# The head of a decoder-layer kernel rebuilt: more warm-up products, a 128-row broadcast of c, the second square on DVE, one inverse root for both row blocks, the bias product moved

## The chip, the cores and the metric

The kernel runs on one core of a Trainium2 chip. The metric is the device time of one execution in microseconds (us). The kernel before was timed three times: 330.17, 328.08 and 331.65 us, median 330.17 us. Engines are named as the profile names them: PE is TensorE's matmul, PEld its weight load, DVE is VectorE, ACT is ScalarE, POOL is GpSimd, SP is SyncE, which here only issues DMAs.

## The reference, cut to what matters

```python
def hybrid_layer(x, c, norm_g, w_ada, b_ada, w_in, ...):
    mod = jax.nn.silu(c) @ w_ada + b_ada
    shift, scale, gate = jnp.split(mod, 3, axis=-1)
    h = rmsnorm(x, norm_g) * (1 + scale[:, None, :]) + shift[:, None, :]
    proj = h @ w_in
    q, k, v, g_attn, cb, cc, cx, g_conv, m_attn, m_conv = jnp.split(proj, IN_OFFSETS, axis=-1)
    attn = moba_attention(split_heads(q), split_heads(k), split_heads(v), rel_bias)
    y_attn = (attn * jax.nn.silu(g_attn)) @ w_o_attn
    y_conv = (short_conv(cb, cc, cx, conv_w) * jax.nn.silu(g_conv)) @ w_o_conv
    merged = jax.nn.sigmoid(m_attn) * y_attn + jax.nn.sigmoid(m_conv) * y_conv
    return x + gate[:, None, :] * (merged @ w_out)
```

The shapes are 256 rows, 1024 channels, 8 heads of 128; all in fp32. A last RMSNorm closes the layer. The change touches only what comes before `h @ w_in`: silu(c), the two sums of squares of x, and the scale and shift of the first 128 channels.

## The kernel before, in words

Rows of x lie on the 128 partitions in two blocks, `xx[:, 0]` and `xx[:, 1]`. The wide products take x transposed: channels on partitions in eight tiles of 128 (`xnT`), 256 rows in the free dimension.

The head does this. PE multiplies a tile of ones by itself (`warm`, L139: four products first, six later), a result nobody reads. It spreads c over all partitions with a product of one row of ones and the row c (`crow`, L225, two products of 512 columns into the banks `pc`), transposes a small table of vectors (`pv`, L227), and after the later warm-ups transposes the scaled x (`px`, L212, sixteen transposes) and makes the bias product (`pb`, L265, from the one-hot table, needed only much later). ACT makes sigmoid(c) half by half (`silu_part`, L233), squares each row block with its sum (`square`, L237), scales each block by its inverse root (L252, L255, L258), copies `px` out and applies scale and shift to the first tile (`full_h(0)`, L165, the tile `hf0`). DVE multiplies sigmoid by c (L234), makes the mean of squares (`rms_scale`, L143), copies the vectors (L242 to L245) and takes the dot products of silu(c) with the rows of w_ada (`ada_dot`, L155), which for one tile end in the reduction into `scs` (L158). POOL raises the mean to the power -0.5 (L145), once for each block.

Then comes the slab stage (`passes`, L205): eight tiles of 128 channels against 2048 columns of w_in, summed in eight PSUM banks. Tile 0 is done wholly in plain fp32 from `hf0` and its slab (16 products of 256 columns), the others mostly as three products of split values. After it the value projection, 36 units of 256 columns with the attention heads between them, the merge and the output projection.

The order on each engine is that of the code, since the head and the slab stage are pinned with `keep_in_program_order`. Loads are issued by SP in the order of the code. An fp32 product shows in the trace as two matmul records, a transpose as one.

Of the kernel before, what the change touches and what calls it, by code (L numbers as in the profile page):

```python
# [23 lines left out]
EPS = 1e-6
NEG = -1.0e30
BLK = {n: i * D for i, n in enumerate(("q", "k", "v", "ga", "cb", "cc", "cx", "gc", "ma", "mc"))}
WARM = 4
WARM2 = 6
EARLYC = 2
# [4 lines left out]
CUTS0 = (0, 2, 3, 4)  # L34
# [9 lines left out]
def layer_kernel(ctx: ExitStack, tc, x, c, vec, wp_all, slab_all, onehot, final_g, out):  # L44
    nc = tc.nc
    x, out = x[0], out[0]

    const = ctx.enter_context(tc.tile_pool(name="const", bufs=1))
    big = ctx.enter_context(tc.tile_pool(name="big", bufs=1))
    wp = ctx.enter_context(tc.tile_pool(name="wp", bufs=3))  # L50
    tp = ctx.enter_context(tc.tile_pool(name="tp", bufs=2))
# [33 lines left out]
    crow = big.tile([1, D], F32, tag="GB", name="crow")  # L85
# [4 lines left out]
    mhalf = const.tile([P, 1], F32, name="mhalf")  # L90
# [25 lines left out]
    pin(nc.sync.dma_start(crow, c))  # L116
# [8 lines left out]
    nc.vector.memset(ones, 1.0)  # L125
# [5 lines left out]
    nc.gpsimd.memset(rv[:, 0:127], NEG)  # L131
    warmup = const.tile([P, 1], F32, name="warmup")
    pin(nc.scalar.activation(warmup, mhalf, AF.Sigmoid))
# [6 lines left out]

    def rms_scale(ss, name):
        ms = tp.tile([P, 1], F32, tag="ms", name=name + "m")
        pin(nc.vector.tensor_scalar(ms, ss, 1.0 / D, EPS, op0=ALU.mult, op1=ALU.add))  # L143
        r = tp.tile([P, 1], F32, tag="rs", name=name + "r")
        nc.gpsimd.tensor_tensor(r, ms, mhalf, op=ALU.pow)  # L145
        return r
# [77 lines left out]
    for n in range(2):  # L224
        pin(nc.tensor.matmul(pc[n], ones[0:1, :], crow[:, n * 512:(n + 1) * 512], start=True, stop=True))  # L225
# [5 lines left out]
    def silu_part(n):  # L231
        cols = slice(n * 512, (n + 1) * 512)
        pin(nc.scalar.activation(csb[:, cols], pc[n], AF.Sigmoid))  # L233
        pin(nc.vector.tensor_mul(csb[:, cols], csb[:, cols], pc[n]))  # L234

    def square(t):
        pin(nc.scalar.activation(xx[:, 2 + t, :], xx[:, t, :], AF.Square, accum_out=ss[:, t:t + 1]))  # L237

    silu_part(0)
    square(0)  # L240
    r0 = rms_scale(ss[:, 0:1], "r0")
    pin(nc.vector.tensor_copy(vT, pv[:, 0:56]))  # L242
    modb = vT[:, 8:24].rearrange("p (k s) -> p k s", s=2)
    pin(nc.vector.scalar_tensor_tensor(modb[:, :, 1], modb[:, :, 1], 1.0, vT[:, 0:KT], op0=ALU.add, op1=ALU.mult))
    pin(nc.vector.tensor_copy(parts[:, :, :, 4], modb))  # L245
    silu_part(1)
    square(1)
    dot = ada_dot(0, CUTS0, 256)
    run(dot, EARLYC)
    r1 = rms_scale(ss[:, 1:2], "r1")  # L250
    run(dot)
    pin(nc.scalar.activation(xx[:, 2, :], xx[:, 0, :], AF.Copy, scale=r0))  # L252
    for k in range(2):
        xn_trans(0, k)
# [9 lines left out]
    pb = wt[0:NH, P:512]  # L264
    pin(nc.tensor.matmul(pb, oneh[:, 3 * P:], oneh[:, 0:3 * P], start=True, stop=True))  # L265
# [409 lines left out]
```

## Time and profile before

| what | value |
|---|---|
| median of three timed runs | 330.17 us (328.08 to 331.65) |
| profiled execution, first to last instruction | 329.4 us |
| PE busy | 321.4 us, 98% |
| DVE busy | 247.3 us, 75% |
| ACT busy | 189.0 us, 57% |
| POOL busy | 5.6 us, 2% |

The profile is of one execution. It gives the span of 329.4 us and no other time for that execution. A busy PE in it is not a PE at its peak: the ends of pipelined matmuls are modelled, so the distance from one start to the next tells more than a duration.

### The profile page before, as it was taken

The numbers are of one execution on the slowest core, as the hardware profiler recorded it, in microseconds if no ns is written. First come the engines' busy times: TensorE is split into PE (matmuls) and PEld (weight loads), VectorE is DVE, ScalarE is ACT, GpSimd is POOL, SyncE is SP. The second block draws the span as 40 slices with busy tenths as digits, with TensorE's granted clock in tenths as the row PEclk, the third lists the DMA queues.
The fourth block names the chain that finished last, engine by engine and source line by source line (L and its number), as shares of the span: only waits on it lengthen the run. The fifth ranks groups of instructions, "written<-read, shape, count | busy, mean of one in ns | idle before, by whom it ended". The sixth has DMA issues, their size and how long they took to land.

```text
span 329.4 us, 4903 instructions
## 1 busy us (share of the span) xinstructions
PE 321.4 (98%) x1870; PEld 281.9 (86%) x1870; DVE 247.3 (75%) x452; ACT 189.0 (57%) x305; POOL 5.6 (2%) x14
## 2 busy tenths in 40 slices
PE   8999999999999999999999999999999999999992
PEld 5689999988888888988888888888888888888892
DVE  2799993476388779697776998999946466787764
ACT  5654555364578676784768574856465635443430
POOL 3000000000000000000000000000000000000010
PEclk9999999999999999999999999999999999999998
DMA  6999999885645434543454469659875665400003
GB/s 240 406 409 403 410 412 352 309 303 214 247 150 200 171 129 141 211 160 127 137 206 169 142 217 373 225 193 370 346 294 205 228 218 202 182 0 2 0 0 127
DMA packets 14264, 72.75 MB, mean 221 GB/s; under 512 B 1523, under 2 KB 2819, under 8 KB 8098
## 3 DMA queue, kind: packets, MB, share of 16 engines
q1 hardware_dynamic: 12658, 70.40, 57.4%
q10 hardware_dynamic: 1488, 1.97, 1.9%
q8 instruction: 14, 0.23, 0.3%
q0 software_dynamic: 96, 0.09, 0.1%
q14 instruction: 8, 0.07, 0.1%
HBM read 71.39 MB, written 1.06 MB: 220 GB/s over the span
## 4 chain that ended last, share of the span: by engine, by line
PE 93%; DMA 2%; DVE 2%; ACT 1%; POOL 1%; SPq 0%; issue 0%; POOLq 0%; DVEq 0%; ACTq 0%
PE acc L205 15%; PE aoa L340 5%; PE acx L340 5%; PE aoc L340 5%; PE acb L340 5%; PE agc L340 5%; PE aga L340 4%; PE amc L340 4%; PE ama L340 4%; PE acc L340 4%; PE aoc L341 2%; PE aoa L341 2%; PE acx L341 2%; PE acc L341 2%; PE acb L341 2%; PE amc L341 2%
## 5 line engine op out<-in xcount | busy, mean ns | idle before, releaser
L205 PE MATMUL acc<-hf,slab 128*128 128x256 f32 x60 | 16.1, 418 | 0.0
L205 PEld LDWEIGHTS acc<-hf,slab 128*128 128x128 f32 x60 | 12.2, 213 | 3.0 <-ACT H L270 1.3
L155 DVE CUSTOM_DVE_ANT_0 ada<-ada,csb,vT 128x512 f32<-128x512 f32 (+1 forms) x18 | 12.3, 687 | 0.0
L155 DVE CUSTOM_DVE_ANT_0 ada<-ada,csb 128x512 f32<-128x512 f32 (+1 forms) x18 | 11.2, 626 | 0.5 <-DMA ada<-in_wp_dram 0.5
L407 DVE CUSTOM_DVE_ANT_0 L<-pS,BI 128x128 f32<-128x128 f32 x8 | 2.3, 292 | 12.2 <-PE pS L404 12.2
L306 DVE TENSOR_SCALAR QK<-acc 128x512 f32<-128x512 f32 x2 | 1.4, 686 | 9.1 <-PE acc L205 9.1
L572 POOL TENSOR_TENSOR rf<-ms,mhalf 128x1 f32<-128x1 f32 x2 | 1.7, 826 | 306.1 <-DVE ms L597 302.5
L554 ACT ACTIVATE SQ<-TT 128x512 f32<-128x512 f32 x3 | 1.9, 626 | 7.6 <-DVE TT L549 7.6
L304 ACT ACTIVATE QK<-acc 128x512 f32<-128x512 f32 x4 | 2.2, 601 | 7.0 <-PE acc L205 7.0
L377 DVE CUSTOM_DVE_ANT_0 gate<-gate,csb,vT 128x512 f32<-128x512 f32 x8 | 6.0, 744 | 0.3 <-DMA gate<-in_wp_dram 0.3
L139 PE MATMUL wt<-ones 128*128 128x128 f32 x20 | 5.0, 437 | 1.0 <-DVE parts L127 1.0
L340 PE MATMUL aoa<-GA,oa0h 128*128 128x512 f32 x16 | 5.8, 404 | 0.0
L340 PE MATMUL aoa<-GA,oa1h 128*128 128x512 f32 x16 | 5.7, 399 | 0.0
L340 PE MATMUL aoc<-GC,oc2h 128*128 128x512 f32 x16 | 5.7, 399 | 0.0
L340 PE MATMUL aoc<-GC,oc1h 128*128 128x512 f32 x16 | 5.7, 399 | 0.0
L340 PE MATMUL aoa<-GA,oa3h 128*128 128x512 f32 x16 | 5.7, 399 | 0.0
L340 PE MATMUL acx<-H,cx0h 128*128 128x512 f32 x16 | 5.7, 398 | 0.0
L340 PE MATMUL aoc<-GC,oc0h 128*128 128x512 f32 x16 | 5.7, 398 | 0.0
L340 PE MATMUL aoa<-GA,oa2h 128*128 128x512 f32 x16 | 5.7, 398 | 0.0
L340 PE MATMUL aoc<-GC,oc3h 128*128 128x512 f32 x16 | 5.7, 398 | 0.0
L340 PE MATMUL acc<-H,cc0h 128*128 128x512 f32 x16 | 5.7, 398 | 0.0
L340 PE MATMUL acb<-H,cb0h 128*128 128x512 f32 x16 | 5.7, 398 | 0.0
(460 smaller groups left out, 1221.9 us busy)
## 6 DMA issues: line engine op xcount, KB each, us to landing
slab<-in_slab_dram SPq DMA_DIRECT2D x16, 512.0 KB, 10.2
ada<-in_wp_dram SPq DMA_DIRECT2D x15, 512.0 KB, 10.2
wv<-in_wp_dram SPq DMA_DIRECT2D x4, 1024.0 KB, 10.6
wcc<-in_wp_dram SPq DMA_DIRECT2D x4, 1024.0 KB, 4.8
wcx<-in_wp_dram SPq DMA_DIRECT2D x4, 1024.0 KB, 4.8
wcb<-in_wp_dram SPq DMA_DIRECT2D x4, 1024.0 KB, 4.8
wgc<-in_wp_dram SPq DMA_DIRECT2D x4, 1024.0 KB, 4.8
wga<-in_wp_dram SPq DMA_DIRECT2D x4, 1024.0 KB, 4.9
```

The lines of the kernel that those rows point to most:

```text
L139: pin(nc.tensor.matmul(wt[:, 0:P], ones, ones, start=True, stop=True))
L155: pin(nc.vector.tensor_tensor_reduce(src, src, csb[:, k:k + n], vT[:, i:i + 1] if s else 1.0, 0.0, ALU.mult, ALU.add, parts[:, i, s, k // ...
L205: pin(nc.tensor.matmul(acc[j // 2][:, (j % 2) * S:(j % 2 + 1) * S], w[i][:, j * P:(j + 1) * P], x, start=(i == 0 and j // 2 not in opened) ...
L304: pin(nc.scalar.activation(dst, src, AF.Copy, scale=scale))
L306: pin(nc.vector.tensor_scalar_mul(dst, src, scale))
L340: nc.tensor.matmul(a, hi[:, k, cols], rhs[:, k, :], start=(k == 0), stop=False)
L341: nc.tensor.matmul(a[:, S:], lo[:, k, cols], rhs[:, k, 0:S], start=False, stop=(k == KT - 1))
L377: nc.vector.tensor_tensor_reduce(src, src, csb[:, q * 512:(q + 1) * 512], 1.0, 0.0 if q else vT[:, 24 + b:25 + b], ALU.mult, ALU.add, gpar ...
L407: nc.vector.tensor_tensor_reduce(L[:, 0:P], pS[:, 0:P], BI[:, h, 0:P][:, ::-1], 1.0, -3.0e38, ALU.add, ALU.max, mx[:, 0:1])
L554: nc.scalar.activation(SQ[:, t, 0:w], TT[:, t, cols], AF.Square, accum_out=s8[:, slot:slot + 1])
L572: nc.gpsimd.tensor_tensor(r, ms, mhalf, op=ALU.pow)
```

## The change

`WARM` goes from 4 to 8 and `WARM2` from 6 to 12; a constant `WARM3` is added that nothing uses. `crow` becomes a tile of 128 rows, cleared by DVE, and c is loaded into its row 0 by ACT's queue and not by SP's; the broadcast multiplies all 128 rows. The square of block 0 stays on ACT and goes ahead of the first sigmoid; that of block 1 becomes one `tensor_tensor_reduce` on DVE. One mean and one power operation of two columns serve both blocks, ahead of the dot products. The vectors are copied by ACT and finished by three POOL operations. The load of tile 0's modulation weights is cut in two and not three, its dot products are 512 columns wide. The bias product is 258 columns wide and stands after the first two transposes.

```diff
-WARM = 4
-WARM2 = 6
-EARLYC = 2
+WARM = 8
+WARM2 = 12
+WARM3 = 2
-CUTS0 = (0, 2, 3, 4)
+CUTS0 = (0, 2, 4)
...
-    crow = big.tile([1, D], F32, tag="GB", name="crow")
+    crow = big.tile([P, D], F32, tag="GB", name="crow")
-    mhalf = const.tile([P, 1], F32, name="mhalf")
+    mhalf = const.tile([P, 2], F32, name="mhalf")
...
-    pin(nc.sync.dma_start(crow, c))
+    nc.vector.memset(ones, 1.0)
+    pin(nc.vector.memset(crow, 0.0))
...
+    pin(nc.scalar.dma_start(crow[0:1, :], c))
...
-        pin(nc.tensor.matmul(pc[n], ones[0:1, :], crow[:, n * 512:(n + 1) * 512], start=True, stop=True))
+        pin(nc.tensor.matmul(pc[n], ones, crow[:, n * 512:(n + 1) * 512], start=True, stop=True))
...
+    pin(nc.scalar.activation(xx[:, 2, :], xx[:, 0, :], AF.Square, accum_out=ss[:, 0:1]))
     silu_part(0)
-    square(0)
-    r0 = rms_scale(ss[:, 0:1], "r0")
-    pin(nc.vector.tensor_copy(vT, pv[:, 0:56]))
+    pin(nc.vector.tensor_tensor_reduce(xx[:, 3, :], xx[:, 1, :], xx[:, 1, :], 1.0, 0.0, ALU.mult, ALU.add, ss[:, 1:2]))
+    ms2 = tp.tile([P, 2], F32, tag="ms2", name="ms2", bufs=1)
+    pin(nc.vector.tensor_scalar(ms2, ss, 1.0 / D, EPS, op0=ALU.mult, op1=ALU.add))
+    r01 = tp.tile([P, 2], F32, tag="r01", name="r01", bufs=1)
+    pin(nc.gpsimd.tensor_tensor(r01, ms2, mhalf, op=ALU.pow))
+    silu_part(1)
+    pin(nc.scalar.activation(vT, pv[:, 0:56], AF.Copy))
     modb = vT[:, 8:24].rearrange("p (k s) -> p k s", s=2)
-    pin(nc.vector.scalar_tensor_tensor(modb[:, :, 1], modb[:, :, 1], 1.0, vT[:, 0:KT], op0=ALU.add, op1=ALU.mult))
-    pin(nc.vector.tensor_copy(parts[:, :, :, 4], modb))
-    silu_part(1)
-    square(1)
-    dot = ada_dot(0, CUTS0, 256)
-    run(dot, EARLYC)
-    r1 = rms_scale(ss[:, 1:2], "r1")
-    run(dot)
-    pin(nc.scalar.activation(xx[:, 2, :], xx[:, 0, :], AF.Copy, scale=r0))
+    pin(nc.gpsimd.tensor_scalar_add(modb[:, :, 1], modb[:, :, 1], 1.0))
+    pin(nc.gpsimd.tensor_mul(modb[:, :, 1], modb[:, :, 1], vT[:, 0:KT]))
+    pin(nc.gpsimd.tensor_copy(parts[:, :, :, 4], modb))
+    run(ada_dot(0, CUTS0, 512))
+    pin(nc.scalar.activation(xx[:, 2, :], xx[:, 0, :], AF.Copy, scale=r01[:, 0:1]))
     for k in range(2):
         xn_trans(0, k)
-    pin(nc.scalar.activation(xx[:, 3, 0:256], xx[:, 1, 0:256], AF.Copy, scale=r1))
+    pb = wt[0:NH, P:512]
+    pin(nc.tensor.matmul(pb[:, 126:], oneh[:, 3 * P:], oneh[:, 126:3 * P], start=True, stop=True))
+    pin(nc.scalar.activation(xx[:, 3, 0:256], xx[:, 1, 0:256], AF.Copy, scale=r01[:, 1:2]))
...
-    pb = wt[0:NH, P:512]
-    pin(nc.tensor.matmul(pb, oneh[:, 3 * P:], oneh[:, 0:3 * P], start=True, stop=True))
```

How the instructions stand, first on PE from its first product to the first slab product (`wt` is the bank of the warm-ups and of the bias product, `acc` the slab stage's). Before:

```order
L139 MATMUL wt<-ones 128x128 x4
L225 MATMUL pc_131<-crow,ones 128x512
L225 MATMUL pc_132<-crow,ones 128x512
L227 MATMUL pv<-ident,vecs 128x56
L139 MATMUL wt<-ones 128x128 x6
L212 MATMUL px_137<-ident,xx 128x128 x4
...
L212 MATMUL px_140<-ident,xx 128x128 x2
L265 MATMUL wt<-oneh 8x384
L205 MATMUL acc_206<-hf_194,slab_95 128x256 x2
```

PE at the same place now:

```order
L140 MATMUL wt<-ones 128x128 x8
L219 MATMUL pc_135<-crow,ones 128x512
L219 MATMUL pc_136<-crow,ones 128x512
L221 MATMUL pv<-ident,vecs 128x56
L140 MATMUL wt<-ones 128x128 x12
L206 MATMUL px_141<-ident,xx 128x128 x2
L248 MATMUL wt<-oneh 8x258
L206 MATMUL px_141<-ident,xx 128x128 x2
...
L206 MATMUL px_144<-ident,xx 128x128 x2
L199 MATMUL acc_209<-hf_197,slab_95 128x256 x2
```

The warm-ups double on both sides of the broadcast, and the bias product leaves the place right ahead of the first slab product.

DVE from its first wait on ACT to the dot products of tile 0, before (`ISA` is a reducing product, the row after it reads its sum):

```order
L234 TENSOR_TENSOR csb<-csb,pc_131 128x512
L143 TENSOR_SCALAR r0m<-ss 128x1
L242 COPY vT<-pv 128x56
...
L234 TENSOR_TENSOR csb<-csb,pc_132 128x512
L155 ISA ada_91,parts<-ada_91,csb 128x256
...
L143 TENSOR_SCALAR r1m<-ss 128x1
L155 ISA ada_91,parts<-ada_91,csb,vT 128x256
```

DVE at the same place now:

```order
L228 TENSOR_TENSOR csb<-csb,pc_135 128x512
L232 ISA xx,ss<-xx 128x1024
L232 ISA ss 128x1
L234 TENSOR_SCALAR ms_161<-ss 128x2
L228 TENSOR_TENSOR csb<-csb,pc_136 128x512
L149 ISA ada_92,parts<-ada_92,csb 128x512
```

The mean of block 1 no longer stands behind the first dot products, which wait for a load; a square of 1024 columns now stands between the first half of silu(c) and both means. On all engines the instructions after the first slab product stand as before.

## Rows read from the trace of the kernel before

**Rows 1.** The page: its first line, the busy time of each engine, the clock row (40 equal slices, tenths of full speed), and the shares of the engines in the chain that ended last.

```profile
span 329.4 us, 4903 instructions
...
PE 321.4 (98%) x1870; PEld 281.9 (86%) x1870; DVE 247.3 (75%) x452; ACT 189.0 (57%) x305; POOL 5.6 (2%) x14
...
PEclk9999999999999999999999999999999999999998
...
PE 93%; DMA 2%; DVE 2%; ACT 1%; POOL 1%; SPq 0%; issue 0%; POOLq 0%; DVEq 0%; ACTq 0%
```

**Rows 2.** What PE waited for in the whole run (the waits of engine PE: total us, times, longest us).

```profile
PE wt L139 <- DVE parts L127: 1.0, 1, 1.0
PE px L212 <- ACT xx L255: 0.7, 1, 0.7
```

**Rows 3.** The chain of waits that ended last, pieces of the first 20 us (start us, us, what).

```profile
0.73 0.34 SPq L116
...
2.00 6.81 DMA ada<-in_wp_dram
...
9.62 0.08 DVE r1m L143
...
9.77 0.73 POOL r1r L145
...
10.52 0.52 ACT xx L255
...
11.08 3.25 PE px L212 x14
14.33 1.37 PE wt L265 x2
```

**Rows 4.** PE in order of time (start us, us, line, what, count): the head; then the slab stage in a window from 15.6 to 19.5 us, then in one from 19.5 to 24.4 us, whose first record began at 19.21.

```profile
1.04 2.08 PE L139 MATMUL wt<-ones 128*128 128x128 f32 x8 [1.04 <-DVE parts L127]
3.05 3.78 PE L225 MATMUL pc<-crow,ones 1*128 1x512 f32 x4
...
7.04 2.93 PE L139 MATMUL wt<-ones 128*128 128x128 f32 x12
9.76 0.63 PE L212 MATMUL px<-ident,xx 128*128 128x128 f32 x2
...
15.63 4.09 PE L205 MATMUL acc<-hf,slab 128*128 128x256 f32 x9
...
19.21 5.48 PE L205 MATMUL acc<-hf,slab 128*128 128x256 f32 x24
24.34 0.47 PE L205 MATMUL acc<-H,slab1h 128*128 128x256 f32 x1
```

**Rows 5.** ACT in order of time in the head.

```profile
0.72 1.28 ACT L133 ACT_TABLE_LOAD   x1 [0.72 <-PEq L664]
...
5.16 0.60 ACT L233 ACTIVATE csb<-pc 128x512 f32<-128x512 f32 x1 [2.94 <-PE pc L225]
...
8.40 1.14 ACT L252 ACTIVATE xx<-xx,r0r 128x1024 f32<-128x1024 f32 x1
...
10.94 0.92 ACT L258 ACTIVATE xx<-xx,r1r 128x768 f32<-128x768 f32 x1
11.81 0.60 ACT L217 ACTIVATE xnT<-px 128x512 f32<-128x512 f32 x1
12.44 0.60 ACT L165 ACTIVATE hf<-xnT,scs 128x256 f32<-128x256 f32 x1
```

**Rows 6.** DVE in order of time in the head (means, products, and the first and last operation of the dot products of tile 1); then groups of DVE's instructions by form in the first 40 us (count, busy us, mean ns).

```profile
5.79 0.69 DVE L234 TENSOR_TENSOR csb<-csb,pc 128x512 f32<-128x512 f32 x1 [4.75 <-ACT csb L233]
6.82 0.15 DVE L143 TENSOR_SCALAR r0m<-ss 128x1 f32<-128x1 f32 x1 [0.35 <-ACT xx L237]
...
15.31 0.69 DVE L155 CUSTOM_DVE_ANT_0 ada<-ada,csb 128x512 f32<-128x512 f32 x1
...
18.00 0.16 DVE L158 TENSOR_REDUCE scs<-parts 128x2 f32<-128x10 f32 x1
...
L155 DVE CUSTOM_DVE_ANT_0 ada<-ada,csb 128x512 f32<-128x512 f32 x10 | 6.8, 684 | 0.0
...
L155 DVE CUSTOM_DVE_ANT_0 ada<-ada,csb 128x256 f32<-128x256 f32 x4 | 1.6, 422 | 0.5 <-DMA ada<-in_wp_dram 0.5
...
L125 DVE MEMSET ones<- 128x128 f32 x1 | 0.2, 165 | 0.8 <-PEq L664 0.8
...
L126 DVE MEMSET mhalf<- 128x1 f32 x1 | 0.1, 59 | 0.0
```

**Rows 7.** DMA issues of the first 60 us: count, KB each, median us from issue to landing.

```profile
xx<-in_x_dram SPq DMA_DIRECT2D x2, 512.0 KB, 3.3
...
oneh<-in_onehot_dram POOLq DMA_DIRECT2D x1, 49.0 KB, 6.7
vecs<-in_vec_dram POOLq DMA_DIRECT2D x1, 28.0 KB, 4.3
```

**Rows 8.** Later in the slab stage, in order of time: ACT's split tile 1 of h, the last slab's split, and PE at that slab.

```profile
18.19 0.60 ACT L165 ACTIVATE H<-xnT,scs 128x256 fp32r<-128x256 f32 x1 [0.66 <-DVE scs L158]
...
51.02 1.06 ACT L187 ACTIVATE slab7h<-slab 128x1024 fp32r<-128x1024 f32 x1 [0.48 <-ACT hf L165]
...
61.98 3.04 PE L205 MATMUL acc<-H,slab7h 128*128 128x256 f32 x24
```

More of the change, by code (lines that the diff above doesn't have):

```diff
@@ L124, in layer_kernel @@
         load_ktile(i)
-    nc.vector.memset(ones, 1.0)
     nc.vector.memset(mhalf, -0.5)
@@ L131, in layer_kernel @@
     nc.gpsimd.memset(rv[:, 0:127], NEG)
+    pin(nc.scalar.dma_start(crow[0:1, :], c))
     warmup = const.tile([P, 1], F32, name="warmup")
-    pin(nc.scalar.activation(warmup, mhalf, AF.Sigmoid))
+    pin(nc.scalar.activation(warmup, mhalf[:, 0:1], AF.Sigmoid))
     wt = bank("wt")
@@ L139, in warm @@
             pin(nc.tensor.matmul(wt[:, 0:P], ones, ones, start=True, stop=True))
[L141 to L146, printed above, removed]
     def ada_dot(i, cuts, n):
@@ L234, in silu_part @@
         pin(nc.vector.tensor_mul(csb[:, cols], csb[:, cols], pc[n]))
-    def square(t):
-        pin(nc.scalar.activation(xx[:, 2 + t, :], xx[:, t, :], AF.Square, accum_out=ss[:, t:t + 1]))
+    pin(nc.scalar.activation(xx[:, 2, :], xx[:, 0, :], AF.Square, accum_out=ss[:, 0:1]))
     silu_part(0)
-    square(0)
-    r0 = rms_scale(ss[:, 0:1], "r0")
-    pin(nc.vector.tensor_copy(vT, pv[:, 0:56]))
-    modb = vT[:, 8:24].rearrange("p (k s) -> p k s", s=2)
-    pin(nc.vector.scalar_tensor_tensor(modb[:, :, 1], modb[:, :, 1], 1.0, vT[:, 0:KT], op0=ALU.add, op1=ALU.mult))
-    pin(nc.vector.tensor_copy(parts[:, :, :, 4], modb))
-    silu_part(1)
-    square(1)
-    dot = ada_dot(0, CUTS0, 256)
-    run(dot, EARLYC)
-    r1 = rms_scale(ss[:, 1:2], "r1")
-    run(dot)
-    pin(nc.scalar.activation(xx[:, 2, :], xx[:, 0, :], AF.Copy, scale=r0))
+    pin(nc.vector.tensor_tensor_reduce(xx[:, 3, :], xx[:, 1, :], xx[:, 1, :], 1.0, 0.0, ALU.mult, ALU.add, ss[:, 1:2]))
[5 more added lines that the diff above has]
+    pin(nc.scalar.activation(vT, pv[:, 0:56], AF.Copy))
+    modb = vT[:, 8:24].rearrange("p (k s) -> p k s", s=2)
+    pin(nc.gpsimd.tensor_scalar_add(modb[:, :, 1], modb[:, :, 1], 1.0))
[3 more added lines that the diff above has]
+    pin(nc.scalar.activation(xx[:, 2, :], xx[:, 0, :], AF.Copy, scale=r01[:, 0:1]))
     for k in range(2):
         xn_trans(0, k)
-    pin(nc.scalar.activation(xx[:, 3, 0:256], xx[:, 1, 0:256], AF.Copy, scale=r1))
+    pb = wt[0:NH, P:512]
+    pin(nc.tensor.matmul(pb[:, 126:], oneh[:, 3 * P:], oneh[:, 126:3 * P], start=True, stop=True))
+    pin(nc.scalar.activation(xx[:, 3, 0:256], xx[:, 1, 0:256], AF.Copy, scale=r01[:, 1:2]))
     for k in range(2):
         xn_trans(1, k)
-    pin(nc.scalar.activation(xx[:, 3, 256:], xx[:, 1, 256:], AF.Copy, scale=r1))
+    pin(nc.scalar.activation(xx[:, 3, 256:], xx[:, 1, 256:], AF.Copy, scale=r01[:, 1:2]))
     xn_copy(0)
@@ L571, in finish @@
         r = tp.tile([P, 1], F32, tag="rs", name=f"rf{t}")
-        nc.gpsimd.tensor_tensor(r, ms, mhalf, op=ALU.pow)
+        nc.gpsimd.tensor_tensor(r, ms, mhalf[:, 0:1], op=ALU.pow)
         pregain(t, cols, src)
```

## The prediction

> **What bounds the kernel now.** I read the page first: PE is busy for 321.4 of 329.4 us and holds 93% of the chain that ended last [rows 1]. Then the waits of PE: two in the whole run, 1.0 us at the start and 0.7 us before the transposes [rows 2]. So once PE has begun the slab stage at 15.63 it does not stop for anything until the output, and what the head can give is the time at which PE is through with slab 0, which was 24.34 [rows 4]. Whatever that moves, the rest should move with it, as long as the producers keep ahead.
>
> They do. Tile 1 of h stood split at 18.19 + 0.60 = 18.79 against its first use at 24.34, and the last slab's split at 51.02 + 1.06 = 52.08 against a use of that slab from 60 to 65 [rows 4, 8]. The lead is 5.5 us at the start and grows. A PE that comes 4 us earlier still finds its data. The dot products of tile 1 (from 15.31 on DVE) stand behind the same work as before, so tile 1 comes at about the old time; this 18.8 is the floor for the end of slab 0.
>
> Next the chain of the head [rows 3]: the load of the first modulation weights until 8.8, two dot products on DVE, and only behind them the mean of block 1 (9.62), its power on POOL (9.77), the scaling on ACT (10.52), fourteen transposes (11.08 to 14.33), the bias product (1.37 us), and the slab stage. The change attacks all of it but the load.
>
> Last the clock. The clock row says full speed in all but the last slice [rows 1], but the starts do not agree. In slab 0 the first eight records start (19.21 - 15.63) / 8 = 0.447 us apart, the next 24 (24.34 - 19.21) / 24 = 0.214 apart [rows 4]: one instruction at the two levels, 1.2 and 2.4 GHz. The head is all at the lower one: 0.251 us for each of the first eight warm-up records (1.04 to 3.05), 0.227 for each of the twelve later ones (7.04 to 9.76), 0.945 for each of the four of the broadcast. Between those warm-ups stood 3.8 us in which only one row of the array worked, and the clock did not rise. It rose some 3.6 to 4 us into the slab products, which use all rows without a gap.
>
> **The change part by part.**
>
> *Warm-ups and broadcast.* Sixteen records at 0.227 to 0.251 from 1.04 on end at 4.7 to 5.05; I take 4.85. Then the broadcast, if c is there. Now it uses 128 rows, so full-row products run without a gap from 1.04 on, and by the delay at slab 0 the clock rises near 5. Before, the first half of the broadcast reached ACT 5.16 - 3.05 = 2.11 us after its start [rows 4, 5]. At the higher level it is half, about 1.05. I take 1.6, between the two, since one rise in one run does not fix its moment: first half at 6.45, against 5.16 before. This part loses 1.3 us, because the warm-ups ahead of c are longer.
>
> *c by ACT's queue.* The load waits for DVE's clearing of `crow`, and the table load and the first square are queued behind it on ACT. The clearing: 0.165 us for 128 columns and 0.059 for one [rows 6] make (0.165 - 0.059) / 127 a column, 0.9 us for 1024; at worst eight times 0.165, 1.3. So it is issued at 1.9 to 2.3. To landing: no more than 2.3 us for the same row before (0.73 to 3.05), 3.3 for x, 4.3 for the vectors [rows 3, 4, 7]. That is 4.2 to 6.6; it is nearest to the same row, so 4.2 to 4.6, just ahead of PE at 4.85. ACT's table load (1.28 us) then ends near 3.7 and the first square (two of x at 3.3 us, now issued first) near 5.3: hidden behind the broadcast.
>
> *Squares, mean, power.* From 6.45: sigmoid to DVE 0.63 (5.16 to 5.79), product 0.69, square of 1024 columns. The same kind of operation takes 422 ns for 256 and 684 for 512 columns [rows 6], so 1.21 for 1024, 1.25 with its reading; mean 0.15; power 0.73, with gaps 0.8. Both roots stand at 9.9. Then ACT scales block 0, 1.14, the first part of block 1, 0.42 (10.52 to 10.94), the rest 0.87 (10.94 to 11.81), copies the transposed x, 0.63, and makes `hf0`, 0.60 [rows 3, 5]: 11.05, 11.5, 12.35, 13.0, 13.6.
>
> *Dot products.* Beside this DVE does the second half of silu(c), 0.69, and four dot products of 512 columns: tile 1's took 18.00 - 15.31 = 2.69, the reduction 0.16 [rows 6]. From 9.15 that is 12.7, ahead of 13.0: hidden by 0.3 us. If that cover went, each further us of it would show whole. The three POOL operations on the vectors have no row like them; between DVE's 0.15 and POOL's 0.73 each they end at 10.4 to 12.1, behind the power in POOL's queue, before the reduction that waits for them. ACT's copy of the vectors falls in its wait for the roots. Two loads for three change no time that anyone waits for, as the last dot products began after 11 before and do now.
>
> *Transposes and bias product.* Fourteen transposes took 3.25 [rows 3]. From 11.5 they end at 14.75 at the old pace, at 13.1 at half; with the clock up I take the half, hidden behind `hf0`. The bias product (1.37 us on the chain) now falls in PE's wait between the two scalings, and its table, among POOL's first instructions and 6.7 us to landing [rows 7], is there before that.
>
> *Slab 0.* It starts at 13.6, 2.0 us earlier, and takes 32 x 0.214 = 6.85 us, not 8.71: 1.9 us. It ends at 20.45, after the floor of 18.8. The sum is 24.34 - 20.45 = 3.9 us. Bounds: broadcast wholly at the higher level 0.55 more, wholly at the lower 0.5 less; transposes at the old pace 14.75 + 6.85 = 21.6, 2.7 us in all. So 2.7 to 4.45.
>
> One rule speaks against leaning on this. The Trainium skill, "TensorE: Matmul & The Clock Gate", Part 4: PE-mode transpose, says that a transpose does not count as a busy PE for the clock. The trace agrees: PE worked without a gap from 11.08, on transposes and a small product, and slab 0 still began at the lower level. By that rule nothing after the last warm-up holds the clock up until slab 0; it is the second rival.
>
> **The rivals.**
>
> *Slower: the clock does not rise in the head.* c fills one row, the other 127 of the broadcast are zeros, and if such a product, or the switching of weights between the products of ones, does not count, all added PE work is done at 1.2 GHz: 4.85 + 3.78 + 0.3 + 24 x 0.227 + 16 x 0.232 + 0.9 = 19.0 for the start of slab 0, and 8.71 more: 27.7, 3.4 us later than now, 332.8. For it: 2.0 and 2.7 us of the same warm-ups did not raise the clock. Against it: now they are 3.8 and, with the broadcast, over 7 us. It decides at a rise later than 16: slab 0 then starts at (19.0 + 16) / 2 = 17.5 and ends 6.85 later, at the old 24.34.
>
> *The clock rises and falls again before slab 0.* From about 10.4 (6.45, 0.95 for the second half, 0.3, 24 x 0.114) to 13.6 PE has transposes, one small product and waits. If that loses the higher level, transposes end at 14.75 and slab 0 at 23.5: 0.9 us gained, 328.5. For it: in the trace the clock row falls in the last slice, after PE's end, and transposes never raised it. Against it: that fall shows only with PE wholly idle.
>
> *c lands late, or the doubled warm-ups leave a gap after all.* With 6.2 in place of 4.2 PE stands for 1.4 us, the broadcast's first half comes at 8.3, `hf0` at 15.4, and slab 0 at the higher level ends at 22.3: 2.0 gained, 327.4; with the rise late as well, about 1 gained.
>
> *It does less than it says:* if PE had waits after 24.34 that the trace gives as work, the gain would stop there. Nothing speaks for that but the modelled ends; I leave it in the remainder.
>
> **How the numbers follow.** The forecast has 0.60, the fall 0.13, late c 0.12, no rise 0.10, the rest 0.05. Against the profiled 329.4 the forecast is 325.5; the median of the runs shown is 0.8 higher, which gives 326.3. I put 326.0. The range reaches from 329.4 - 4.45, 325, with a little for the spread of the runs, 324.8, to the two middle rivals, 328.5 with the 0.8, rounded to 329.5; that holds the forecast, the fall and the late c, 0.85. One per cent, what a measurement of this kernel can tell from no change, is 3.3 us: 326.9 and 333.5. The forecast's 2.7 to 4.45 lies astride the first, some three quarters of it beyond: 0.45 for faster. A quarter of the forecast, the fall, late c and most of the rest are no change: 0.44. No rise, 332.8 to 333.6, with the remainder: 0.11 slower.
>
> **What would show it.** Warm-up records 0.25 apart that fall to about half near 5 to 8 us, and the later 24 within 3 us; broadcast starting at 4.8 to 5 with no gap; the one power operation at 9.1; slab 0 from 13.6, all 32 records 0.214 apart, done near 20.5; no new wait of PE behind it. Wrong would be: warm-ups at 0.227 to the end and slab 0 at 19, the no-rise rival; slab 0 beginning with records 0.45 apart after fast warm-ups, the fall; a wait of PE for `crow`, the late load; a wait of PE at tile 1 or later, which would say that the lead was not what I read.

## The result, and the profile after

The changed kernel takes 331.51 us (median of 20 runs, 329.79 to 333.39), the kernel before 329.45 us (20 runs, 327.0 to 333.46). The ratio is 1.0078 with a 95% interval of 1.0052 to 1.0104: slower, by 2.1 us between the medians, and within about one per cent, where 326.0 was forecast. The first lines of its page, against [rows 1]:

```profile
span 329.7 us, 4933 instructions
...
PE 319.6 (97%) x1890; PEld 280.9 (85%) x1890; DVE 248.2 (75%) x443; ACT 188.6 (57%) x304; POOL 6.8 (2%) x16
...
PEclk9899999999999999999999999999999999999999
...
PE 94%; DMA 1%; issue 1%; DVE 1%; ACT 0%; POOL 0%; POOLq 0%; ACTq 0%
```

PE is busy 1.8 us less and the span is 0.3 us longer. The clock row has a dent in its second slice that [rows 1] lacks. What PE waited for, against [rows 2]:

```profile
PE pc L219 <- DMA crow<-in_c_dram: 2.6, 1, 2.6
PE wt L140 <- DVE ones L116: 1.0, 1, 1.0
```

The broadcast waits 2.6 us for c. The chain of waits shows what stands ahead of it (start us, us, what):

```profile
1.15 0.91 DVE crow L117
...
2.09 4.90 DMA crow<-in_c_dram
...
7.13 3.48 PE pc L219 x4
```

The clearing takes the 0.91 us that was forecast, but the load of one row lands at 6.99, not at 4.2 to 4.6. PE in order of time (start us, us, line, what, count; the row of the slab stage is from a window of 12 to 21 us, the last from the view of one tile, whose columns are durations min/median/max in ns and first to last start in us):

```profile
1.04 3.45 PE L140 MATMUL wt<-ones 128*128 128x128 f32 x16 [1.04 <-DVE ones L116]
7.13 3.48 PE L219 MATMUL pc<-crow,ones 128*128 128x512 f32 x4 [2.64 <-DMA crow<-in_c_dram]
...
10.82 2.94 PE L140 MATMUL wt<-ones 128*128 128x128 f32 x24
...
14.56 1.75 PE L206 MATMUL px<-ident,xx 128*128 128x128 f32 x14
...
16.32 5.01 PE L199 MATMUL acc<-hf,slab 128*128 128x256 f32 x22
...
L199 PE MATMUL acc<-H,slab1h x24: 278/283/467, 23.1 to 28.8; 128*128 128x256 f32 x24
```

The sixteen early warm-ups end at 4.49, PE stands until 7.13, and the broadcast then takes 3.48 us, little less than the 3.78 of [rows 4]. The trace's clock record says why: the clock rose at 3.99, fell at 7.41 and rose again at 10.82. One stretch of the table by windows (columns: PE, PEld, DVE, ACT, POOL busy and counts, clock, DMA share, GB/s) has it at the lower level, with PE busy throughout:

```profile
7.41:10.82 3.41, 3.41 (x6) 0.85 (x4) 1.25 (x2) 0.77 (x2) 0.00 (x0) 0.50 1.00 379
```

Slab 0 then starts at 16.32, and slab 1 at 23.14, 1.2 us ahead of the 24.34 of [rows 4]. That lead does not reach the end: from there to the end of the span it is 306.5 us, against 305.1 before. PE has no further wait, so only its pace can have eaten it. In the 36 units each pair of products has 512 and 256 columns. Here are the products of 512 columns of two units in the kernel before (gc2 and mc3), then of the same two and of oc3 in the changed one:

```profile
L340 PE MATMUL agc<-H,gc2h x16: 392/394/395, 177.9 to 183.1; 128*128 128x512 f32 x16
L340 PE MATMUL amc<-H,mc3h x16: 392/394/395, 250.0 to 255.2; 128*128 128x512 f32 x16
```

```profile
L332 PE MATMUL agc<-H,gc2h x16: 395/398/403, 176.6 to 181.9; 128*128 128x512 f32 x16
L332 PE MATMUL amc<-H,mc3h x16: 395/398/403, 250.1 to 255.4; 128*128 128x512 f32 x16
...
L332 PE MATMUL aoc<-GC,oc3h x16: 395/398/403, 295.4 to 300.7; 128*128 128x512 f32 x16
```

From gc2 to mc3, thirteen units of the same work, it is 72.1 us before and 73.5 now. The lead of 1.3 us at gc2 is gone at mc3. By the starts in the trace a pair takes 346.5 ns in one kernel and 353.3 in the other, all the way from gc1 to oa0: 83.3 against 84.9 us, 1.6 us. So two things are to be explained: a head that came 2.7 us later than forecast, and a later pace that nobody had touched.

### The profile page after: what moved, and what is told of

It reads as the page before. It is cut to its first block, busy times and chain, and to the rows that moved or that the text cites. A ratio compares the mean times of both kernels' runs of the same rounds, so it can differ in the third digit from the quotient of the medians.

```text
span 329.7 us, 4933 instructions
## 1 busy us (share of the span) xinstructions
PE 319.6 (97%) x1890; PEld 280.9 (85%) x1890; DVE 248.2 (75%) x443; ACT 188.6 (57%) x304; POOL 6.8 (2%) x16
## 3 DMA queue, kind: packets, MB, share of 16 engines
HBM read 71.39 MB, written 1.06 MB: 220 GB/s over the span
## 4 chain that ended last, share of the span: by engine, by line
PE 94%; DMA 1%; issue 1%; DVE 1%; ACT 0%; POOL 0%; POOLq 0%; ACTq 0%
PE acc L199 15%; PE ama L332 5%; PE amc L332 5%; PE aoc L332 5%; PE aoa L332 5%; PE aga L332 5%; PE acx L332 5%; PE agc L332 5%; PE acc L332 5%; PE acb L332 4%; PE acx L333 2%; PE ama L333 2%; PE aoc L333 2%; PE aoa L333 2%; PE aga L333 2%; PE amc L333 2%
## 5 line engine op out<-in xcount | busy, mean ns | idle before, releaser
L149 DVE CUSTOM_DVE_ANT_0 ada<-ada,csb,vT 128x512 f32<-128x512 f32 x16 | 12.0, 749 | 0.0
L149 DVE CUSTOM_DVE_ANT_0 ada<-ada,csb 128x512 f32<-128x512 f32 x16 | 11.0, 688 | 0.0
L159 ACT ACTIVATE H<-xnT,scs 128x256 fp32r<-128x256 f32 x7 | 4.2, 604 | 5.8 <-DVE scs L152 5.8
L140 PEld LDWEIGHTS wt<-ones 128*128 128x128 f32 x40 | 6.0, 240 | 1.1 <-DVE ones L116 1.0
L332 PE MATMUL agc<-H,gc1h 128*128 128x512 f32 x16 | 5.8, 404 | 0.0
L332 PE MATMUL agc<-H,gc2h 128*128 128x512 f32 x16 | 5.7, 399 | 0.0
L332 PE MATMUL aga<-H,ga1h 128*128 128x512 f32 x16 | 5.7, 399 | 0.0
L332 PE MATMUL ama<-H,ma0h 128*128 128x512 f32 x16 | 5.7, 399 | 0.0
L332 PE MATMUL ama<-H,ma3h 128*128 128x512 f32 x16 | 5.7, 399 | 0.0
L332 PE MATMUL amc<-H,mc2h 128*128 128x512 f32 x16 | 5.7, 399 | 0.0
```

What stands on the lines that cost most here:

```text
L140: pin(nc.tensor.matmul(wt[:, 0:P], ones, ones, start=True, stop=True))
L149: pin(nc.vector.tensor_tensor_reduce(src, src, csb[:, k:k + n], vT[:, i:i + 1] if s else 1.0, 0.0, ALU.mult, ALU.add, parts[:, i, s, k // ...
L159: pin(nc.scalar.activation(dst, xnT[:, i, :], AF.Identity, scale=scs[:, i, 1:2], bias=scs[:, i, 0:1]))
L332: nc.tensor.matmul(a, hi[:, k, cols], rhs[:, k, :], start=(k == 0), stop=False)
```

## The experiments

Two theories stood at first: the late c (the head decides) and the pace (the stretch from gc1 on decides). The rival to both was that the two profiles were just unlike executions.

**The two kernels, looked at again** (before_again and after_again are copies, no edit).

> The kernel before, unchanged, for a second trace of it. Theory 'pace' (after the head PE falls into one of two paces, 346.5 or 353.5 ns for a pair of products of 512 and 256 columns, and which stretch runs at which pace differs from one execution to the next): slab 1 begins within 1.5 us of 24.3, yet the stretch from the first gc1 product to the first oa0 product is either 83.3 us, as in the first trace, or 84.9, and the span differs from 329.4 by the sum of such differences. Theory 'late c' (all that matters is when slab 0 is done): the span less the start of slab 1 is again 305.1 within 0.3.

> The changed kernel, unchanged, for a second trace. Both theories: the row c lands near 7.0 again, 4.9 us after its issue, and PE waits about 2.6 us for it. 'Pace': the span less the start of slab 1 (306.6 in the first trace) differs by up to 2 us between the two traces of the same program. 'Late c': it is 306.6 within 0.3, and the time varies with the clock in the head alone.

Medians 331.0 (327.15 to 331.97) and 331.74 (330.45 to 333.81) against 329.52 for the kernel before on the same chip: ratios 1.0028 (0.9983 to 1.0073) and 1.009 (1.0057 to 1.0124). The stretch from gc1 to oa0 was 83.3 and 84.9 us again. The pace belongs to the program, not to the execution. The clock of the head does not: in after_again it did not rise until 12.45, and slab 0 began at 17.08, not at 16.32.

**c first, one row** (c_first_row: the changed kernel with c back at the front of SP's queue and the broadcast of one row).

```diff
-    crow = big.tile([P, D], F32, tag="GB", name="crow")
+    crow = big.tile([1, D], F32, tag="GB", name="crow")
-    pin(nc.vector.memset(crow, 0.0))
+    pin(nc.sync.dma_start(crow, c))
-    pin(nc.scalar.dma_start(crow[0:1, :], c))
-        pin(nc.tensor.matmul(pc[n], ones, crow[:, n * 512:(n + 1) * 512], start=True, stop=True))
+        pin(nc.tensor.matmul(pc[n], ones[0:1, :], crow[:, n * 512:(n + 1) * 512], start=True, stop=True))
```

> The changed kernel with c loaded as one row by SP ahead of all other loads and the broadcast made from that one row, as before the change; warm-ups, square on DVE, one root, bias product as changed. 'Late c': c lands by 3, PE starts the broadcast at 4.5 without a wait, the first half reaches ACT at about 6.6 or, at the higher clock, 5.6, the first slab product starts at 13 to 14 in place of 16.3, slab 1 begins at 20 to 22 in place of 23.1, and the median falls 1.5 to 3 us below the changed kernel's. 'Pace': the head ends as early as that, but the median moves by less than 1 us, as the stretches after it run at the slow pace. A third reading, that one-row products lose the clock: the first slab records are 0.45 apart and slab 1 begins at 22 to 23.

PE in order of time, and a stretch by windows:

```profile
4.48 1.98 PE L218 MATMUL pc<-crow,ones 1*128 1x512 f32 x4
...
6.59 4.57 PE L139 MATMUL wt<-ones 128*128 128x128 f32 x24
...
13.61 0.70 PE L198 MATMUL acc<-hf,slab 128*128 128x256 f32 x2
```

```profile
7.54:10.96 3.42, 3.42 (x18) 3.42 (x18) 2.35 (x7) 1.81 (x3) 1.37 (x4) 0.50 1.00 393
```

The gap is gone and slab 0 starts at 13.61, as forecast for the change itself. Yet the median is 331.18 (328.71 to 331.71), ratio 1.0037 (0.9992 to 1.0083): the spans lie at 326.8 to 327.2 in three executions, the traced one among them, and at 329.3 to 329.8 in seven. The stretch from gc1 to oa0 is again 84.9. The clock fell from 7.54 to 10.96 although PE had no gap.

**c by 128 rows of DMA** (c_wide: each partition loads c, no broadcast on PE, both sigmoids ahead of the first square, 20 and 4 warm-ups).

```diff
-    pin(nc.vector.memset(crow, 0.0))
+    pin(nc.sync.dma_start(crow, bass.AP(tensor=c.tensor, offset=c.offset, ap=[[0, P], [1, D]])))
...
-WARM = 8
-WARM2 = 12
+WARM = 20
+WARM2 = 4
```

> The changed kernel with c loaded on all 128 partitions by SP ahead of all other loads (0.5 MB), no broadcast on PE, warm-ups 20 and 4. 'Late c': sigmoid of c starts near 3.7, the roots stand near 8.5, the first slab product starts near 12 and slab 1 begins at 19 to 20, four us earlier than in the changed kernel; the median is 325.5 to 327.5. 'Pace': slab 1 as early, the median above 328.

332.19 (331.44 to 333.42), ratio 1.0088 (1.0052 to 1.0123). The load puts 512 KB ahead of x; the square of block 1 waited for x until 8.1, and PE stood 2.85 us before the first transposes:

```profile
12.07 0.44 PE L205 MATMUL px<-ident,xx 128*128 128x128 f32 x2 [2.85 <-ACT xx L240]
...
13.39 3.25 PE L205 MATMUL px<-ident,xx 128*128 128x128 f32 x14
```

The clock fell at 12.43, and the fourteen transposes went at the lower level. In this form, with the tiles at their lower place and 20 and 4 warm-ups, a wide load saves nothing against the changed kernel's 331.74.

**What sets the pace: the place of tiles.** Against the kernel before, the changed one has every tile of one pool that is made after the head (hf, low, E, ET, L, cc, cx, y) 64 bytes lower in SBUF, since two small tiles of one buffer each stand in the place of two with two buffers each. Five runs take this apart. b_sbuf is the kernel before with that shift alone, its order of work kept:

```diff
+    ms2 = tp.tile([P, 2], F32, tag="ms2", name="ms2", bufs=1)
+    r01 = tp.tile([P, 2], F32, tag="r01", name="r01", bufs=1)
     def rms_scale(ss, name):
-        ms = tp.tile([P, 1], F32, tag="ms", name=name + "m")
+        t = int(name[1])
+        ms = ms2[:, t:t + 1]
...
-        r = tp.tile([P, 1], F32, tag="rs", name=name + "r")
+        r = r01[:, t:t + 1]
```

> The kernel before with one edit: the two inverse roots write two columns of shared tiles, so that the pool's later tiles (hf, low, E, ET, L, cc, cx, y) lie 64 bytes lower in SBUF, as they do in the changed kernel; the order of the work is that of before. The head should stay as it was: slab 1 from about 24.2. Theory layout (where the tiles lie sets which of two paces PE falls into after the attention's last product): gc1 to oa0 takes 84.9 us instead of 83.3, time about 331 to 332. Theory entry (how long the program before it is, and when the stretch is entered, sets the pace): 83.3, time that of before, 329.5. Theory chance (each execution falls anew into either pace): either, and the spread of the executions is that of before, 326.9 to 331.6.

a_layout is the changed kernel with the shift taken back:

```diff
-    ms2 = tp.tile([P, 2], F32, tag="ms2", name="ms2", bufs=1)
+    ms2 = tp.tile([P, 2], F32, tag="ms2", name="ms2", bufs=2)
...
-    r01 = tp.tile([P, 2], F32, tag="r01", name="r01", bufs=1)
+    r01 = tp.tile([P, 2], F32, tag="r01", name="r01", bufs=2)
```

> The changed kernel with two spare buffers of 32 bytes, so that the pool's later tiles lie where they lay in the kernel before; nothing else. Head as in the changed kernel: slab 1 from 23.1 to 23.9. Theory layout: gc1 to oa0 takes 83.3 us, time about 330.0, 1.6 us under the changed kernel's 331.6. Theory entry: 84.9, time 331.6. Theory chance: either.

Products of 512 columns in gc2 and mc3, b_sbuf and then a_layout:

```profile
L344 PE MATMUL agc<-H,gc2h x16: 395/398/403, 174.0 to 179.3; 128*128 128x512 f32 x16
L344 PE MATMUL amc<-H,mc3h x16: 395/398/403, 247.5 to 252.8; 128*128 128x512 f32 x16
```

```profile
L332 PE MATMUL agc<-H,gc2h x16: 392/394/395, 176.3 to 181.5; 128*128 128x512 f32 x16
L332 PE MATMUL amc<-H,mc3h x16: 392/394/395, 248.4 to 253.6; 128*128 128x512 f32 x16
```

73.5 us with the tiles lower, 72.1 with them back. The times follow: b_sbuf 330.48 (328.87 to 331.49), ratio 1.004 (0.9999 to 1.0082); a_layout 330.0 (329.31 to 331.54), ratio 1.0031 (0.9993 to 1.007), 1.5 us under the changed kernel. Over all runs without added products, seven traces with the tiles at the old place have 83.3 us from gc1 to oa0 and six with them lower have 84.9. Which of the shifted tiles carries it was not tried.

**More warm-ups alone** (b_warm).

```diff
-WARM = 4
-WARM2 = 6
+WARM = 8
+WARM2 = 12
```

> The kernel before with 8 and 12 warm-up products instead of 4 and 6, nothing else; layout and order are those of before, PE has 10 products more. Head: the broadcast waits for 16 warm-up records and begins at about 4.5 instead of 3.05, so the DVE and ACT chain starts up to 1.4 us later; if the clock rises at about 4.2 as in the run with c first, slab 0 runs at 0.213 (6.8 us instead of 8.7) and slab 1 begins at 23.5 to 24.3; if it falls again before slab 0, slab 1 begins at about 25.7. Theory layout: gc1 to oa0 83.3. Theory entry: it may be 84.9. Time 329 to 331 by the first, 331 to 333 by the second.

328.76 (327.24 to 330.36), ratio 0.9989 (0.9944 to 1.0034), 83.3 us from gc1 to oa0. Ten products more on PE do not change the pace, so the theory of entry falls. Slab 0 began at 13.55, as early as c_first_row managed, and the median still did not move. That was the first sign that the early slab 0 might be nothing new to the kernel before.

**Can a break choose the pace?** (a_breaks: one product of 256, 128, 64 or 32 columns ahead of each half of every unit.)

```diff
+            w = (256, 128, 64, 32)[len(breaks) % 4]
+            breaks.append(name)
+            nc.tensor.matmul(a[:, 0:w], hi[:, 0, cols], rhs[:, 0, 0:w], start=True, stop=True)
             for k in range(KT):
```

> The changed kernel with one more product ahead of each half of every unit (all 72 halves, 256, 128, 64 and 32 columns in turn), written to a bank that the next product starts anew: the output is the same. It asks whether the pace is chosen at a break in the row of pairs of 512 and 256 columns, and can be chosen by the break's length. Theory entry or layout for the whole stretch: gc1 to oa0 stays at one pace, 353 ns a pair in all halves, and the run is longer by the products alone (72 x 0.03 to 0.11, some 5 us). If each break chooses anew: halves at 346.5 and halves at 353.3 are found in the same stretch, by width if the length decides, mixed within a width if not.

337.15 (two runs). PE behind a break of 128 columns, and behind one of 32 (first product of each pair):

```profile
181.73 0.40 PE L337 MATMUL agc<-H,gc2h 128*128 128x512 f32 x1
...
182.09 0.40 PE L337 MATMUL agc<-H,gc2h 128*128 128x512 f32 x1
...
182.44 0.40 PE L337 MATMUL agc<-H,gc2h 128*128 128x512 f32 x1
...
182.79 0.40 PE L337 MATMUL agc<-H,gc2h 128*128 128x512 f32 x1
...
187.57 0.39 PE L337 MATMUL agc<-H,gc3h 128*128 128x512 f32 x1
...
187.91 0.39 PE L337 MATMUL agc<-H,gc3h 128*128 128x512 f32 x1
...
188.26 0.39 PE L337 MATMUL agc<-H,gc3h 128*128 128x512 f32 x1
```

1.06 us for three pairs and 0.69 for two. In the trace all 18 halves behind 32 columns go at 346 to 347 ns a pair, and so do 17 of the 18 behind 64 columns and 13 of the 18 behind 256; 13 of the 18 behind 128 columns go at 353. Both kinds stand in one stretch, and mostly, not wholly, by width. So the pace is a state that a break sets and that lasts until the next one.

**Two breaks, and the pace is back** (a_relock: the changed kernel, tiles lower, with two products of 32 columns).

```diff
+            if t == 1 and name in ("gc1", "oa0"):
+                nc.tensor.matmul(a[:, 0:32], hi[:, 0, cols], rhs[:, 0, 0:32], start=True, stop=True)
             for k in range(KT):
```

> The changed kernel, its layout untouched, with two more products of 32 columns, one ahead of the second half of gc1 and one ahead of the second half of oa0, each into a bank that the next product starts anew. In the run with a product ahead of every half, all halves behind one of 32 columns went at 346.5 ns a pair. If the pace is a state that a break sets and that lasts to the next one, gc1 to oa0 falls from 84.9 to about 83.5 us, the eight oa and oc units from 5.65 to 5.54 us each (0.8 in all), and the time by about 2.1 us, to about 329.4. If the pace is kept by the addresses themselves, it falls back behind the two products: gc1 to oa0 84.9 and 331.6.

329.28 (328.97 to 330.26), 329.4 expected; ratio 1.0029 (0.9993 to 1.0064).

```profile
L334 PE MATMUL agc<-H,gc2h x16: 391/391/392, 176.4 to 181.6; 128*128 128x512 f32 x16
...
L334 PE MATMUL aoc<-GC,oc3h x16: 391/391/392, 293.1 to 298.3; 128*128 128x512 f32 x16
```

From gc1 to oa0 it is now 83.5 us, and behind it 0.75 us less than in the changed kernel. So the addresses do not hold the pace: with the tiles where they were, one product of 32 columns gives the faster one for the rest of the stretch. Two products that compute nothing save 2.2 us of the changed kernel's time.

**Both losses taken out** (c_first_layout is c_first_row with the spare buffers of a_layout; v_row has the two products of a_relock besides).

> The changed kernel with both suspects taken out: c loaded first, as one row on the queue of SP (the broadcast has one row again, and there is no zeroing of the 128 rows), and two spare buffers of 32 bytes that put the pool's later tiles where they lay before. Head as in the earlier run with c first: slab 0 from 13.6. gc1 to oa0 83.3. If late c and the tiles' place are the two losses, the time is 331.2 - 1.6 = 329.6 by the median of that run and 327.2 by its three best executions. If it stays at 331 the place of the tiles is not what the executions without a trace lost.

> c loaded first as one row, the old place of the tiles, and the two products of 32 columns: a version meant to beat both. It should read as the run with c first and the old place, with gc1 to oa0 at 83.4 and oa0 to ao 0.7 us shorter: 328.9 by the median, 326.5 by the best. If the clock still comes late in most executions, its spread has two groups 2.5 us apart.

329.59 (327.42 to 330.33), ratio 1.0005 (0.9963 to 1.0046), and 329.39 (326.89 to 329.93), ratio 0.9988 (0.9947 to 1.003). Each has two groups of spans, 325.5 to 325.8 and 327.8 to 328.6 in the first, 325.0 to 325.2 and 327.4 to 328.0 in the second. The profile of v_row fell in the later group: the clock rose only at 13.81, and the same broadcast of one row took 3.78 us, not 1.98:

```profile
4.76 3.78 PE L218 MATMUL pc<-crow,ones 1*128 1x512 f32 x4
...
16.53 7.17 PE L198 MATMUL acc<-hf,slab 128*128 128x256 f32 x32
```

**c early into 128 rows** (a_c_early: the changed kernel with this edit alone, three more early warm-ups included; v_128: with the spare buffers and the two products too).

```diff
-    pin(nc.vector.memset(crow, 0.0))
+    pin(nc.vector.memset(crow[:, 0:512], 0.0))
+    pin(nc.gpsimd.memset(crow[:, 512:], 0.0))
+    pin(nc.scalar.dma_start(crow[0:1, :], c))
     pin(nc.sync.dma_start(xx[:, 0, :], x[0:P, :]))
...
-    pin(nc.scalar.dma_start(crow[0:1, :], c))
...
-WARM = 8
+WARM = 11
```

> The changed kernel, its layout of the pool and its pace untouched, with c loaded earlier: its 128 rows are zeroed half by DVE and half by POOL, the load goes out at about 1.5 instead of 2.1 on the queue of ACT, and 11 instead of 8 products stand ahead of the broadcast, so that no gap is left. c should land at 5.3, the broadcast begin at 5.9 instead of 7.1, slab 0 at 14.2 instead of 16.3, with no fall of the clock in the head. If late c is worth what slab 0's start says, 1.8 to 2.1 us, the time is 329.6 with a narrow spread, and gc1 to oa0 stays at 84.9. If the two losses are not independent, it stays above 330.5.

> The other version: c into 128 rows as in the change, but the zeroing is split between DVE and POOL, so that the load is issued at about 1.5 instead of 2.1 on the queue of ACT, 11 instead of 8 products ahead of the broadcast, the old place of the tiles, the two products of 32 columns. By the queue (vecs issued at 1.27 served at 4.76, crow issued at 2.09 served at 6.37) c should land at about 5; the broadcast runs from 5.1, with 128 rows, and slab 0 begins at 13.6 to 14.5. If 128 rows keep the clock up where one row lost it, there is no fall in the head and the time is 326 to 327.5 in most executions. If the row count does not matter, it is that of the version with one row, or 0.6 more.

PE in a_c_early, then in v_128:

```profile
5.64 1.88 PE L220 MATMUL pc<-crow,ones 128*128 128x512 f32 x4
...
14.07 7.17 PE L200 MATMUL acc<-hf,slab 128*128 128x256 f32 x32
```

```profile
5.75 1.88 PE L220 MATMUL pc<-crow,ones 128*128 128x512 f32 x4
...
14.18 7.17 PE L200 MATMUL acc<-hf,slab 128*128 128x256 f32 x32
```

No fall of the clock in either head (rise at 5.35 and 5.59). a_c_early takes 329.69 (329.06 to 330.09), ratio 0.9993 (0.9958 to 1.0028): 1.8 us under the changed kernel by the medians, 2.25 by the starts of slab 0. v_128 takes 327.47 (327.06 to 328.07), ratio 0.9958 (0.9924 to 0.9991), and its ten spans lie within 1.1 us, 325.2 to 326.3.

**Was the early slab 0 there all along?** (before_3 and before_4, copies of the kernel before, one execution each.)

> The kernel before, looked at once more. If the groups of its spans are the clock's: an execution with a span of 325 to 326.5 shows a rise of the clock at about 10, slab 0 from 13.8 (as the same order of work showed in the run with the tiles 64 bytes lower), slab 1 from 20.6 and the stretch gc1 to oa0 at 83.3; one with 329 to 330 shows the rise at about 19 and slab 1 from 24.2. If they are not the clock's, a span of 325 to 326.5 goes with slab 1 from 24.2 and a shorter later stretch.

> The same once more, since which group an execution falls into is not ours to choose: the same two readings.

before_3, then before_4: the page's first line, the fourteen transposes, slab 0, the first products of slab 1 (in before_3 from a window that starts at 24.4).

```profile
span 329.7 us, 4903 instructions
...
11.63 3.25 PE L212 MATMUL px<-ident,xx 128*128 128x128 f32 x14 [1.24 <-ACT xx L255]
...
16.19 8.72 PE L205 MATMUL acc<-hf,slab 128*128 128x256 f32 x32
...
24.56 1.30 PE L205 MATMUL acc<-H,slab1h 128*128 128x256 f32 x8
```

```profile
span 325.9 us, 4903 instructions
...
11.52 1.75 PE L212 MATMUL px<-ident,xx 128*128 128x128 f32 x14 [1.17 <-ACT xx L255]
...
13.94 7.17 PE L205 MATMUL acc<-hf,slab 128*128 128x256 f32 x32
...
20.77 0.47 PE L205 MATMUL acc<-H,slab1h 128*128 128x256 f32 x1
```

One program, the transposes started within 0.1 us of each other, and the difference is the clock: it rose at 19.35 in the one and at 10.19 in the other. Slab 1 began at 24.56 and at 20.77, and the spans differ by the same 3.8 us. The execution on which the prediction rests was of the first kind: its clock rose at 19.47. Of 108 executions of the kernel before in the four timed jobs, 54 have spans up to 326.6, the kind of before_4; 23 have 329.1 or more; 31 lie between, at 327.2 to 328.5, and have no trace.

**All repairs, and two more edits** (v_best: v_128 with the square of block 1 ahead of the product with c's first half on DVE, and 9 warm-ups).

```diff
-WARM = 11
+WARM = 9
...
-    silu_part(0)
     pin(nc.vector.tensor_tensor_reduce(xx[:, 3, :], xx[:, 1, :], xx[:, 1, :], 1.0, 0.0, ALU.mult, ALU.add, ss[:, 1:2]))
+    silu_part(0)
```

> The version of the run before with c into 128 rows early, the old place of the tiles and the two products of 32 columns, with two more edits: the square of the second row block on DVE stands ahead of the product with c's first half (it has 1.14 us there and waited for nothing but x), and 9 instead of 11 products stand ahead of the broadcast. If DVE's row (mul 0.69, square 1.14, root, mul, four dots of 0.72) sets the head, slab 0 begins 1.1 to 1.6 us earlier, at 12.6 to 13.1, and the time is 325.9 to 326.4. If the load of ada0, which lands at about 9.1, or slab 1's data set it, slab 0 begins no earlier than 13.6 or PE waits behind slab 0, and the time stays at 327.0 to 327.5. If the shorter row of products lets the clock fall, 328 or more.

327.37 (326.54 to 328.33), ratio 0.9921 (0.988 to 0.9962) against 329.45 in its job. Its median is that of v_128; the ratio is lower because only 6 of 21 executions of the kernel before had spans up to 326.6 in its job, and 18 of 31 in that of v_128. Slab 0 began at 13.77, not at 12.6 to 13.1: the 24 later warm-up records held PE until 11.2, while the first block of x stood scaled at 10.84, so PE's own row, not DVE's, set the transposes. It takes 4.1 us less than the changed kernel; against the kernel before its gain is under one per cent.

## Why the prediction was wrong

The measured median lies 5.5 us above the forecast of 326.0, and the trace divides this: slab 1 began 2.7 us later than forecast (23.14 against 20.45), the work behind it took 1.5 us more than before (306.5 against 305.1), and 1.3 us are the step from the profile to the timed runs.

**c's landing was mis-sized.** The step was "it is nearest to the same row, so 4.2 to 4.6". The clearing (0.9 forecast, 0.91) and the issue (1.9 to 2.3, 2.09) were right. But the same row had stood first in line, and now x and the first weights stood ahead of it on SP's queue. The nearest row was that of the vectors, 4.3 us from issue to landing behind the same loads [rows 7], which gave the upper bound of 6.6; it took 4.90. In five traces with the same issue it took 4.20 to 4.90, so this trace had the longest. Half a microsecond of earlier issue was worth 1.0 to 1.7 us of landing: in v_best the chain has

```profile
1.62 3.69 DMA crow<-in_c_dram
```

The rival "c lands late" had the mechanism and its chance of 0.12 was far too low. It forecast the first half of the broadcast at 8.3 and the end of slab 0 at 22.3; they came at 8.94 and 23.14, because c landed at 6.99 and not at the 6.2 that it took. The lower clock of the broadcast was in its 8.3 already, which is 2.1 us after 6.2. Landing c earlier, with the 11 warm-ups that this allows, gives back 1.8 us (331.51 to 329.69).

**"Whatever that moves, the rest should move with it"** failed in a way no wait shows. The lead of producers was read rightly, and PE did not wait behind slab 0. But the same products ran 2% slower for 84 us, because two small tiles were given one buffer instead of two and the rest of the pool lies 64 bytes lower for it. That costs 1.5 to 1.6 us. The remainder rival, that the gain would stop after 24.34 in something that the trace gives as work, had the right place but another mechanism: it spoke of hidden waits, and here the products themselves came further apart. The rows gave no sign of it: a price of this kind is not to be read from a trace of before.

**The base was one kind of execution.** "What the head can give is the time at which PE is through with slab 0, which was 24.34" took one rise of the clock for a property of the kernel. I wrote that one rise in one run does not fix its moment, and applied it to the new head only. In before_4 it is through with slab 0 at 20.77, and by the spans so it is in half of its executions (that those without a trace are of this kind is inferred): there 3.6 of the 3.9 us were not to be had. The three timed runs shown, 328.08 to 331.65, were spread by 3.6 us, and I made nothing of it. Nor is a span a time: in every run here the time of an execution is 1.7 to 1.9 us above its span, so the profiled 329.4 is a time of about 331.2 (an estimate), one of the slowest kind. I set it beside the median of 330.17, added 0.8 and then rounded down to 326.0. A span of 325.5 would have been about 327.3, which is the 1.3 us. The Trainium skill, "TensorE: Matmul & The Clock Gate", Part 1: The HAM clock gate (the "warmup" mystery), says that the point at which the clock rises differs between runs of one kernel. The traces agree: 19.35 and 10.19 in before_3 and before_4.

**What was right.** The warm-ups ended at 4.49 (4.85 forecast) and the clock rose ahead of the broadcast (near 5 forecast, 3.99). From the first half of the broadcast to `hf0` it was 7.3 us (7.15 forecast), and slab 0 took 6.82 us (6.85). The single terms held, too; against [rows 5, 6]:

```profile
10.17 1.22 DVE L232 CUSTOM_DVE_ANT_0 xx<-xx 128x1024 f32<-128x1024 f32 x1
...
15.66 0.60 ACT L159 ACTIVATE hf<-xnT,scs 128x256 f32<-128x256 f32 x1
```

The square was forecast at 1.21. Fourteen transposes took 1.75 us, about half of 3.25, as forecast with the clock up. The dot products stayed hidden. The second rival, a fall before slab 0, came only in part: the clock fell at 7.41, was back at 10.82 and stayed up through the transposes into slab 0. Whether transposes count for the clock no run here shows.

**The sum.** 331.5 less 1.8 for late c and 1.5 for the tiles' place is 328.2, an estimate from two single repairs; v_128 without its 0.7 us in the oa and oc units gives the same. The kernel before had medians of 328.0 to 329.5 in its five sets of 20 to 31 runs, and 331.0 in one of ten. So by the larger sets the head as designed, with both accidents repaired, is worth between nothing and 1.3 us, and what it brings is a narrow spread rather than a lower floor.

## What to carry to other kernels

Look at several executions before you price a head that depends on the clock: what the worse kind of execution loses is no gain of the change. Price a small load by what is queued ahead of it on every queue, not by how long the same bytes took when they were first. And after any edit that adds or drops a tile, compare the pace of the long stretches far from the edit; if it has changed, a tile of padding or one short product may bring it back.

## What the runs showed of the hardware

- Pairs of products of 512 and 256 columns have two stable paces, 346.5 and 353.3 ns, at one clock. A 64-byte shift of tiles that PE does not read in that stretch decided between them in 13 of 13 traces, and one product of 32 columns ahead of a half led to the faster one in 18 of 18. Why is open.
- A 4 KB load on ACT's queue, issued at 2.1, took 4.20 to 4.90 us in five traces behind loads on SP's queue, and 3.69 us when issued half a microsecond earlier. Its packet began when SP's queue had moved about 1.2 MB (the changed kernel, at 6.13) and 1.0 MB (v_best, at 4.68); x has 1.0 MB. The Trainium skill, "DMA: Bandwidth & Descriptors", Queues, rings and completion order, says that a DMA engine takes turns between the queues it has work for. By that one would expect the row to pass x. The traces do not agree: its packet began only when as many bytes as x has had gone by, as if all queues stood in one line. Why is not shown.
- With c in one row, PE without a gap lost the clock at 7.54 (until 10.96) in c_first_row, and the spans fell into two groups. With 128 rows and c early (a_c_early, v_128, v_best; PE's longest waits after its start 0.6, 0.8 and 0.2 us) no trace shows a fall, and the spans of a_c_early and v_128 lie within 1.1 us each. That the row count is the cause was not isolated: c's queue and the early warm-ups changed with it. With 128 rows and late c, the clock fell behind waits of 2.6 and 2.4 us (the changed kernel, a_relock), stayed up behind one of 1.9 (a_breaks), and in after_again and a_layout it had not yet risen when c came.
